# A mixture-of-experts kernel on Trainium2: the first expert weights laid out in the order in which they are fetched

## The chip, the cores and the metric

The kernel runs on one core of a Trainium2 chip. The metric is the device time of one execution in microseconds (us), as the median of several runs. The engines are PE (TensorE: matrix multiplies), DVE (VectorE), ACT (ScalarE), POOL (GpSimd) and SP (SyncE, which issues almost all transfers); 16 DMA engines move the data. All numbers are 32-bit floats unless said otherwise.

## What is computed

A batch of one, 256 tokens of width 1024, goes through two layers of a first model (three kinds of mixers and a dense feed-forward part) and then through one layer of a second model (attention and a recurrent mixer, then a mixture of 32 experts). The change touches the experts' weights alone. What they compute:

```python
def moe_ffn(h, ...):                     # h: 256 tokens x 1024
    logits = hf @ w_router + b_router    # 32 experts, the best 4 of each token
    ...
    def expert_block(args):
        xb, e = args
        gu = xb @ w_gu[e] + b_gu[e]      # w_gu[e]: 1024 x 2048, gate and up
        gate = jnp.minimum(gu[:, :D_EXPERT], SWIGLU_LIMIT)
        up = jnp.clip(gu[:, D_EXPERT:], -SWIGLU_LIMIT, SWIGLU_LIMIT)
        glu = gate * jax.nn.sigmoid(SWIGLU_ALPHA * gate)
        return ((up + 1.0) * glu) @ w_down[e] + b_down[e]   # w_down[e]: 1024 x 1024
    ...                                  # weighted by the gates and summed per token
```

"First weights" are `w_gu`, "second weights" `w_down`. The weights are inputs, and the program reads each expert's weights once: 32 x (8 + 4) MB.

## The kernel before

The first two layers and the second model's mixer come first, with their own weights. The last part, `moe`, goes over the 32 experts one after the other. Each expert has 24 units of weights, 512 KB each, a unit being one tile of 128 partitions x 1024 numbers: 8 units for each half `fh` of the first product (rows `kk` of 128, of the gate columns and of the up columns 512 each), then 8 units of second weights (rows of 128, all 1024 columns). `first` multiplies up to 64 gathered tokens with 8 units, `swiglu` applies the gate, `second` multiplies with the last 8, and the results of two experts are scattered back together. The experts at places 10, 16 and 22 in the order get 2, 1 and 1 extra blocks of 64 tokens (`HEAVY`, function `more`), which use the same units while they are held. Before the last expert stands a branch (`missing`, L2401) for tokens that found no place.

The units pass through a ring (`Ring`, from L1718). `ring_slots` lists the tiles of the earlier stages whose room is used again: 34 units in all (the tiles `rw2`, `rows`, `xh`, `xl`, `t`, `raw`, `hi`, `lo`, `mh`, `ml`, `cst1`; in the profile `rw`, `cst` and so on). `Ring.fill` is called after each group of matmuls and issues units up to 34 ahead. SP takes these issues in program order: each waits until PE has finished with the slot's former unit, and until the transfer eight before it has landed, since the transfers go over eight semaphores in turn. The experts' order is known only at run time; for every six experts `Ring.who` loads their numbers into registers of SP (L1754), and an issue adds the offset to the address. `Ring.fetch` issues one unit: for units 0 to 15 the source is 128 rows of `w_gu[e]`, of each row two pieces of 512 numbers (2 KB), 4 KB apart; for units 16 to 23 the source is 128 rows of `w_down[e]`, 1024 numbers (4 KB) each, one behind the other. `Ring.bias` issues an expert's 8 KB of biases.

The function `layout` prepares the inputs on the host, outside of the timed execution.

Of the kernel before, what the change touches and what calls it, by code (L numbers as in the profile page):

```python
# [20 lines left out]
P = 128  # L21
S = 256
D = 1024
KT = D // P
# [4 lines left out]
NE = 32  # L29
# [15 lines left out]
def _pair_rows(base):  # L45
    return np.concatenate([np.arange(base + h * 64, base + h * 64 + 64) for j in range(4) for h in PAIRS[j]])


def _in_columns():
    g, r, n = 0, 1040, 2096  # L50
    z = -1
    cols = []
    cols += list(range(r + 768, r + 896))
    cols += list(range(r + 896, r + 1024))
    cols += list(range(r + 1024, r + 1056))
    cols += list(range(g + 1024, g + 1040)) + [z] * 16
    cols += list(range(n + 1280, n + 1304)) + [z] * 8
    cols += list(range(3400, 3432))
    cols += list(range(r + 256, r + 512))
    cols += list(range(r, r + 256))  # L60
    cols += list(range(r + 512, r + 768))
    cols += list(range(g, g + 512))
    cols += list(range(g + 768, g + 1024))
    cols += list(_pair_rows(n))
    cols += list(range(n + 512, n + 768))
    cols += list(range(n + 768, n + 896))
    cols += list(range(n + 1024, n + 1152))
    cols += list(range(g + 512, g + 768))
    cols += list(range(n + 896, n + 1024))
    cols += list(range(n + 1152, n + 1280))  # L70
    return np.array(cols)
# [146 lines left out]
def _blocks(w):  # L218

    return np.ascontiguousarray(w.reshape(KT, P, -1, P).transpose(2, 1, 0, 3))  # L220


def layout(inp):
    inp = {k: np.asarray(v) for k, v in inp.items()}
    cols = _in_columns()
    o = {}
    o["xtm"] = inp["x"][0]
    o["xT"] = np.ascontiguousarray(inp["x"][0].T)
    for l in range(2):
        w = np.concatenate([inp["w_in"][l], inp["w_in_vres"][0] if l else np.zeros((D, 32), np.float32),  # L230
                            np.zeros((D, 1), np.float32)], 1)[:, cols]
        o[f"win{l}"] = _blocks(w[:, :NFM * P])

        wt = w[:, NFM * P:].reshape(2, 4, P, 2, 256)
        o[f"wtm{l}"] = np.ascontiguousarray(wt.transpose(3, 0, 2, 1, 4))
        gu = np.stack([inp["ffn_w_gate"][l].reshape(D, NFB, P), inp["ffn_w_up"][l].reshape(D, NFB, P)], 2)
        o[f"wgu{l}"] = _blocks(gu.reshape(D, 2 * FF))
        o[f"wdn{l}"] = np.ascontiguousarray(inp["ffn_w_down"][l])
        rows = np.concatenate([np.arange(512), _pair_rows(512)])
        o[f"wo{l}"] = np.ascontiguousarray(inp["w_out"][l][rows])  # L240
        o[f"wc{l}"] = np.ascontiguousarray(np.stack([inp["nsa_wk1"][l], inp["nsa_wv1"][l]]))
        o[f"pos{l}"] = np.concatenate([inp["nsa_pos_k"][l].reshape(16, P), inp["nsa_pos_v"][l].reshape(16, P)], 0)
        o[f"rows{l}"] = np.stack([inp["gla_ln_w"][l], inp["gla_ln_b"][l], inp["rwkv_ln_w"][l], inp["rwkv_ln_b"][l]])
        o[f"ln{l}"] = np.stack([inp["ln1_w"][l], inp["ln1_b"][l], inp["ln2_w"][l], inp["ln2_b"][l]])
    c2 = np.concatenate([_pair_rows(0), np.arange(512, 1792)])
    o["win2"] = _blocks(inp["w_in_2"][0][:, c2])
    rows = np.concatenate([_pair_rows(0), np.arange(512, 1024)])
    o["wo2"] = np.ascontiguousarray(inp["w_out_2"][0][rows])
    o["wada"] = inp["w_ada_2"][0]
    o["bada"] = inp["b_ada_2"]  # L250
    o["g3"] = np.stack([inp["g_mix_2"][0], inp["g_ffn_2"][0], inp["g_final_2"]])
    o["wgu"] = inp["w_gu_2"][0]
    o["wdn"] = inp["w_down_2"][0]

    o["bgu"] = np.ascontiguousarray(inp["b_gu_2"][0].reshape(NE, 2, KT, P).transpose(0, 3, 2, 1).reshape(NE, P, KT * 2))
    o["bdn"] = inp["b_down_2"][0]
    pr, _ = params(inp)
    o["pfm"] = np.ascontiguousarray(np.concatenate(pr.parts, 1))
    o["cst"] = np.ascontiguousarray(np.concatenate(CONST.parts, 1).astype(np.float32))
    return o, pr  # L260
# [1457 lines left out]
class Ring:  # L1718
# [37 lines left out]

    def fetch(self, w, u, es):
        k, d = self.k, self.k.d
        if u < 16:
            fh, kk = divmod(u, KT)  # L1760
            src = d["wgu"][es, kk * P:(kk + 1) * P, :].rearrange("o p (g f c) -> f (o p) g c", g=2, f=2)[fh]
            k.nc.sync.dma_start(w.rearrange("p (g c) -> p g c", g=2), src)
        else:
            k.nc.sync.dma_start(w, d["wdn"][es, (u - 16) * P:(u - 15) * P, :].rearrange("o p c -> (o p) c"))

    def bias(self, b, es):

# [804 lines left out]
```

## Time and profile before

| | |
|---|---|
| time, median of 3 runs | 2018.57 us (2015.73 to 2022.04) |
| the profiled execution | 2017.36 us, span 2015.6 us |
| PE / DVE / ACT / POOL busy in it | 1856.2 / 954.7 / 536.2 / 495.5 us |
| DMA | 571.82 MB in 234584 packets, 284 GB/s over the span |
| shares of the chain that ended last | PE 43%, DMA 21%, DVE 5%, ACT 3%, POOL 3% |
| mean granted TensorE clock | 0.968 of full speed |

The span runs from the first to the last instruction of the profiled execution; the execution's own time holds some 2 us more. Busy time is summed over stages that have different limits, so a share of the span says little about any one stage. The DMA share is the mean busy share of the 16 DMA engines; it passes 1 where the records of packets overlap. The chain is followed back from the last instruction: at each step to what released it.

### The profile page before, as it was taken

The numbers are of one execution on the slowest core, as the hardware profiler recorded it, in microseconds if no ns is written. First come the engines' busy times: TensorE is split into PE (matmuls) and PEld (weight loads), VectorE is DVE, ScalarE is ACT, GpSimd is POOL, SyncE is SP. The second block draws the span as 40 slices with busy tenths as digits, with TensorE's granted clock in tenths as the row PEclk, the third lists the DMA queues.
The fourth block names the chain that finished last, engine by engine and source line by source line (L and its number), as shares of the span: only waits on it lengthen the run. The fifth ranks groups of instructions, "written<-read, shape, count | busy, mean of one in ns | idle before, by whom it ended". The sixth has DMA issues, their size and how long they took to land.

```text
span 2015.6 us, 32453 instructions
## 1 busy us (share of the span) xinstructions
PE 1856.2 (92%) x12219; PEld 1137.0 (56%) x12219; DVE 954.7 (47%) x1705; ACT 536.2 (27%) x977; POOL 495.5 (25%) x425
## 2 busy tenths in 40 slices
PE   8989999999998999898799988999999999999886
PEld 7867899888867998697333322333333323332222
DVE  3656777667566776667433222233323322332222
ACT  4424444444343444364311100101111101110011
POOL 2434499234552995204200000000000000000000
PEclk9889999999898999998799999999999999999998
DMA  7420578754314778457899999969999999999997
GB/s 273 158 77 31 185 271 274 247 168 138 106 53 148 245 264 290 146 168 237 328 390 395 391 392 392 390 226 393 392 394 390 394 390 391 392 382 394 390 393 268
DMA packets 234584, 571.82 MB, mean 284 GB/s; under 512 B 22179, under 2 KB 31843, under 8 KB 234421
## 3 DMA queue, kind: packets, MB, share of 16 engines
q1 hardware_dynamic: 234420, 569.68, 78.0%
q8 instruction: 98, 1.61, 0.3%
q14 instruction: 66, 0.53, 0.1%
HBM read 568.54 MB, written 1.07 MB: 283 GB/s over the span
## 4 chain that ended last, share of the span: by engine, by line
PE 43%; DMA 21%; DVE 5%; ACT 3%; POOL 3%; issue 2%; SPq 0%; POOLq 0%; ACTq 0%; DVEq 0%
PE ps L385 41%; DMA raw<-wgu 4%; DMA t<-wgu 3%; DVE t L318 3%; DMA lo<-wgu 2%; PE ps L389 2%; ACT t L318 2%; DMA hi<-wgu 1%; POOL acc L318 1%; DMA cst<-wgu 1%; DMA mh<-wgu 1%; DVE lo L318 1%; DMA mh<-wdn 1%; DMA ml<-wgu 1%; POOL ada L318 1%
## 5 line engine op out<-in xcount | busy, mean ns | idle before, releaser
L385 PE MATMUL ps<-t,t 128*128 128x128 bf16 (+13 forms) x3912 | 452.0, 324 | 34.4 <-DVE t L318 12.2
L318 DVE TENSOR_TENSOR lo<-raw,hi 128x1024 fp32r<-128x1024 f32 x187 | 296.3, 1607 | 152.8 <-ACT hi L318 152.6
L318 ACT COPY t<-ps 128x512 f32<-128x512 f32 (+4 forms) x196 | 101.3, 525 | 861.6 <-PE ps L385 791.7
L385 PE MATMUL ps<-xh,hi 128*128 128x256 f32 x1184 | 310.5, 297 | 10.7 <-ACT hi L318 10.7
L385 PE MATMUL ps<-xh,lo 128*128 128x256 f32 x1184 | 305.5, 293 | 13.0 <-DVE lo L318 13.0
L385 PEld LDWEIGHTS ps<-t,t 32*32 32x32 f32 (+4 forms) x3000 | 176.1, 141 | 212.7 <-issue 119.4
L318 POOL TENSOR_SCALAR t<-t 128x1 f32<-128x1 f32 (+2 forms) x24 | 9.9, 411 | 1162.8 <-DVE t L318 1162.6
L318 DVE TENSOR_TENSOR t<-ps,pfm 128x512 f32<-128x512 f32 (+1 forms) x108 | 74.4, 688 | 414.0 <-PE ps L389 228.5
L318 ACT CAST hi<-raw 128x1024 fp32r<-128x1024 f32 x224 | 229.3, 1048 | 101.4 <-PE ps L385 50.8
L385 PEld LDWEIGHTS ps<-xh,lo 128*128 128x128 f32 x1184 | 238.2, 201 | 17.5 <-DVE lo L318 15.9
L385 PEld LDWEIGHTS ps<-xh,hi 128*128 128x128 f32 x1184 | 238.1, 201 | 15.5 <-ACT hi L318 10.9
L385 PE MATMUL ps<-xl,hi 128*128 128x256 f32 x1184 | 167.9, 285 | 0.0
L318 DVE TENSOR_TENSOR x<-x,ps 128x512 f32<-128x512 f32 x80 | 54.3, 686 | 212.9 <-PE ps L385 212.8
L385 PEld LDWEIGHTS ps<-xl,hi 128*128 128x128 f32 x1184 | 155.0, 195 | 0.0
L318 POOL TENSOR_TENSOR acc<-acc,ada 128x1024 f32<-128x1024 f32 x48 | 127.1, 2647 | 5.6 <-DMA acc<-bada 1.8
L318 POOL TENSOR_TENSOR lo<-raw,hi 128x1024 fp32r<-128x1024 f32 x37 | 93.3, 2522 | 125.6 <-ACT hi L318 102.8
L318 POOL TENSOR_SCALAR ada<-ada,cpar 128x1024 f32<-128x1024 f32 x48 | 114.6, 2387 | 36.7 <-DMA ada<-wada 36.6
L385 PE MATMUL ps<-hi,t 128*64 128x512 f32 x424 | 100.1, 599 | 3.7 <-DMA hi<-wgu 3.7
L385 PE MATMUL ps<-raw,t 128*64 128x512 f32 x416 | 97.9, 598 | 4.5 <-DMA raw<-wgu 4.1
L385 PE MATMUL ps<-lo,t 128*64 128x512 f32 x416 | 97.1, 597 | 3.2 <-DMA lo<-wgu 3.2
L389 PE MATMUL ps<-cst,t 128*128 128x128 f32 x524 | 85.1, 281 | 11.9 <-ACT t L318 9.5
L389 PEld LDWEIGHTS ps<-cst,t 128*128 128x128 f32 x524 | 58.4, 142 | 63.4 <-issue 34.2
(190 smaller groups left out, 2202.7 us busy)
## 6 DMA issues: line engine op xcount, KB each, us to landing
raw<-wgu SPq DMA_DIRECT2D x148, 512.0 KB, 5.6
t<-wgu SPq DMA_DIRECT2D x122, 512.0 KB, 10.5
raw<-wdn SPq DMA_DIRECT2D x76, 512.0 KB, 10.1
raw<-win SPq DMA_DIRECT2D x60, 512.0 KB, 4.3
hi<-wgu SPq DMA_DIRECT2D x60, 512.0 KB, 9.4
t<-wdn SPq DMA_DIRECT2D x58, 512.0 KB, 10.0
lo<-wgu SPq DMA_DIRECT2D x56, 512.0 KB, 10.6
ada<-wada SPq DMA_DIRECT2D x48, 512.0 KB, 4.3
```

Of the source, the lines that this page charges most:

```text
L318: r = f(*args, **kw)
L385: self.clk.note("PE", "mm", [out, lhsT, rhs], cost, self.nc.tensor.matmul(out, lhsT, rhs, start=start, stop=stop, skip_group_check=True))
L389: self.clk.note("PE", "tr", [out, in_], 110.0, self.nc.tensor.transpose(out, in_, ident))
```

## The change

The host lays out the first weights so that each unit is one run of 512 KB, in which each partition's 1024 numbers (512 of the gate, 512 of the up columns) lie one behind the other. The dimensions become expert, unit (`fh` outside, `kk` inside), partition, number. `w_down` is only given the same four dimensions; its bytes stay where they are. `Ring.fetch` then takes a unit by its number, with one form for both kinds. A transfer of first weights now reads 128 pieces of 4 KB where it read 256 pieces of 2 KB. The order of instructions on every engine, the slots, the waits and the registers are the same as before; lines behind the edit have other numbers.

```diff
-    o["wgu"] = inp["w_gu_2"][0]
-    o["wdn"] = inp["w_down_2"][0]
+
+    o["wgu"] = np.ascontiguousarray(inp["w_gu_2"][0].reshape(NE, KT, P, 2, 2, 512).transpose(0, 4, 1, 2, 3, 5)).reshape(NE, 16, P, 1024)
+    o["wdn"] = inp["w_down_2"][0].reshape(NE, KT, P, D)
...
     def fetch(self, w, u, es):
         k, d = self.k, self.k.d
-        if u < 16:
-            fh, kk = divmod(u, KT)
-            src = d["wgu"][es, kk * P:(kk + 1) * P, :].rearrange("o p (g f c) -> f (o p) g c", g=2, f=2)[fh]
-            k.nc.sync.dma_start(w.rearrange("p (g c) -> p g c", g=2), src)
-        else:
-            k.nc.sync.dma_start(w, d["wdn"][es, (u - 16) * P:(u - 15) * P, :].rearrange("o p c -> (o p) c"))
+        src = d["wgu"][es, u] if u < 16 else d["wdn"][es, u - 16]
+        k.nc.sync.dma_start(w, src.rearrange("o p c -> (o p) c"))
```

## Rows read from the trace of the kernel before

**Rows 1.** The page's 40 slices: busy tenths of the DMA engines, and GB/s.

```profile
DMA  7420578754314778457899999969999999999997
GB/s 273 158 77 31 185 271 274 247 168 138 106 53 148 245 264 290 146 168 237 328 390 395 391 392 392 390 226 393 392 394 390 394 390 391 392 382 394 390 393 268
```

**Rows 2.** The chain of waits, 900 to 2016 us: start, duration, what.

```profile
1021.05 9.80 PE ps L385 x80
...
1123.31 9.80 PE ps L385 x80
...
1138.88 11.37 DMA raw<-wgu
...
1258.47 3.87 PE ps L385 x52
...
1466.17 9.80 PE ps L385 x80
...
1548.38 9.80 PE ps L385 x80
...
1579.98 11.41 DMA lo<-wgu
...
1687.36 1.10 PE ps L385 x4
...
1799.35 7.96 DMA raw<-wgu
...
1969.92 6.25 DMA xh<-wgu
1976.29 9.19 PE ps L385 x32
```

**Rows 3.** Stretches of the expert stage: busy times; last, PEclk, DMA share, GB/s.

```profile
1008.00:1258.00 250.00, 234.33 (x1154) 80.29 (x1150) 71.68 (x148) 24.33 (x47) 4.96 (x4) 1.00 1.04 392
1258.00:1332.00 74.00, 68.94 (x386) 27.13 (x386) 20.63 (x44) 9.35 (x18) 0.00 (x0) 1.00 1.03 388
1332.00:1351.00 19.00, 17.96 (x74) 5.94 (x72) 7.04 (x12) 0.74 (x2) 0.00 (x0) 1.00 0.02 9
1351.00:1969.00 618.00, 586.76 (x3026) 210.52 (x3022) 174.58 (x366) 63.30 (x124) 0.00 (x0) 1.00 1.04 390
```

**Rows 4.** DMA queues over 1612–1620, 1629–1637, 870–875, 500–505, 630–635 us.

```profile
DMA packets 1634, 3.08 MB, mean 385 GB/s; under 512 B 138, under 2 KB 138, under 8 KB 1633
q1 hardware_dynamic: 1633, 3.06, 104.2%
...
DMA packets 979, 3.28 MB, mean 410 GB/s; under 512 B 101, under 2 KB 101, under 8 KB 979
q1 hardware_dynamic: 979, 3.28, 103.5%
...
DMA packets 702, 2.01 MB, mean 401 GB/s; under 512 B 62, under 2 KB 62, under 8 KB 702
...
DMA packets 1552, 1.86 MB, mean 371 GB/s; under 512 B 68, under 2 KB 1437, under 8 KB 1552
...
DMA packets 568, 1.71 MB, mean 342 GB/s; under 512 B 61, under 2 KB 189, under 8 KB 568
q1 hardware_dynamic: 568, 1.71, 99.0%
```

**Rows 5.** SP's issues in order of time: start, duration, engine, transfer, count.

```profile
988.37 0.54 SPq L318 DMA_DIRECT2D rows<-wgu  x1
...
1032.06 0.33 SPq L318 DMA_DIRECT2D rows<-wdn  x1
...
1324.80 26.38 SPq L318 DMA_DIRECT2D hi<-wgu  x4
```

**Rows 6.** Waits of SP's queue: us in total, times, longest.

```profile
SPq L318 <- DMA t<-wgu: 73.7, 113, 1.5
```

**Rows 7.** PE's loads of weights behind the branch, in order of time, with the idle time.

```profile
1976.26 0.32 PEld L385 LDWEIGHTS ps<-t,t 128*64 128x64 f32 x4 [7.57 <-PEq L2401]
```

## The prediction

> **What bounds the kernel now.** I read the 40 slices first, to find where the transfers are at their limit. From slice 21 on (about 1008 us) the 16 DMA engines are busy nine tenths or more in all slices but two, the one at the seventh place of that stretch and the last, and move about 390 GB/s [rows 1]. That is the expert stage; before it the rate never stays there. Next the chain of waits, to see whether the end hangs on those transfers. In the expert stage it changes hands six times [rows 2]: PE until 1138.9, transfers until 1258.5, PE until 1580.0, transfers until 1687.4, PE until 1799.4, transfers until 1976.2, then PE to the end. The reader should see two paces in it. Where PE leads, the same piece (9.80 us, x80) comes back every 51.13 us (1021.05, 1123.31 with one between): two experts, 25.57 us each. Where an expert has an extra block of tokens it takes longer: 82.21 us from 1466.17 to 1548.38, so 31.1 us for one extra block. The transfers' pace follows from the view by stages [rows 3]: at 392 GB/s an expert's 24 units of 524,288 bytes take 32.1 us. PE is thus faster by 6.5 us per expert. It lives off the ring of 34 units, runs it empty, and waits; each expert with extra blocks (10, 16, 22) lets the ring fill again. Once it fills to the brim: the queue stands still from 1332 to 1351 [rows 3], in one issue of four units that takes 26.38 us [rows 5].
>
> Last I looked at what the queue moves at which rate, in stretches in which nearly all pieces have one size [rows 4]. Over 1612 to 1620 it is the first weights: 1633 pieces for 3.06 MB (138 of them tiny), about 2 KB each, 385 GB/s. Over 1629 to 1637 it is mostly second weights, 4 KB pieces: 979 pieces, 410 GB/s. Both at a DMA share above 1, so in neither did the engines lack work.
>
> **The change, part by part.** No instruction is added, removed or moved on any engine: the same 768 units go to the same slots in the same order, PE reads the same bytes. What changes is the source of 512 of them (16 per expert): 256 pieces of 2 KB become 128 of 4 KB, as the 256 units of second weights have now.
>
> *A unit of first weights.* Now 524,288 B / 385 GB/s = 1.362 us. For the new form I take the rate of the units that already have it, 410 GB/s: 1.279 us. The difference is 0.083 us. Bounds: the other stretch with almost only 4 KB pieces lies in the first layer's stage, 401 GB/s [rows 4], which gives 1.307 us and a difference of 0.055; below that, nothing, if piece size is not the cause (a rival). I take 410 because it is the same stage, the same queue depth and the same kind of source; 0.055 goes to the range.
>
> *How many of them lie on the path.* Two stretches.
> - From 1008 to 1258 the queue never stops: 250 us x 392 GB/s = 98.0 MB, 187 units, two thirds of them first weights: 125. 125 x 0.083 = 10.3 us. They make expert 10 begin earlier. PE could go along: it needs 51.1 us for two experts, and the new transfers would take 48 x 1.279 = 61.4, so transfers stay the later ones.
> - From 1258 to 1351 PE leads while the ring fills and then stands. Nothing is gained here: the 74 us of transfers are covered by PE's extra blocks. The queue restarts when PE frees a slot, so its restart moves with PE, by 10.3 us. If that cover were gone, these units would be worth 74 x 388 / 524 = 55 units, 37 x 0.083 = 3 us.
> - From 1351 to 1969 it never stops again: 618 us x 390 GB/s = 241 MB, 460 units, 306 first weights, 306 x 0.083 = 25.4 us.
> - The units fetched before 1008 lie behind PE's own chain up to 1138.9: nothing (at most some 36 units, 3 us, if it were otherwise).
> - SP's issue of a unit: 0.54 us now, 0.33 for the 4 KB form [rows 5]. Nothing: SP waits for landings of earlier units before it issues (113 times for one tile alone, 0.65 us each [rows 6]), so a shorter issue only lengthens that wait. These waits also show what is late next if a unit came slower: the issue behind it.
>
> *What may eat some of it: the ring.* Gain that PE can't use at once, as in the PE stretches 1351 to 1580 and 1687 to 1799, stays as units ahead, unless the ring is full. At 1351 it holds 34. To 1540 the queue brings 189 us x 390 / 524 = 140 units; PE eats (189 - 31.1) / 25.57 = 6.2 experts, 148 units: 26 are left. The change adds 140 x 2/3 x 0.083 / 1.279 = 6, so 32 of 34. At the end of expert 22 the like could be a few more if PE took nothing of the gain between; four units over would cost 4 x 1.279 = 5 us. I count nothing for it and give 5 us to the range.
>
> *The end.* After the last transfer wait PE loses 7.57 us at the branch ahead of the last expert [rows 7] and then runs alone for 27 us; neither changes.
>
> **Sum.** 10.3 + 25.4 = 35.7 us off the profiled execution: span 2015.6 to 1979.9, its own time 2017.4 to 1981.7. The median of the runs, 2018.57, lies 1.2 above that execution, so for a median: **1983 us**.
>
> **The rivals.**
>
> *Only part of the difference is piece size.* The stretch 500 to 505 moved 1.86 MB in 1552 - 68 pieces, 1253 bytes each, at 371 GB/s [rows 4]. Each engine moves a sixteenth, so such a piece takes 54.0 ns and one of 2 KB (at 385) 85.1 ns; the line through these two has 5.0 ns per piece, and puts 4 KB at 165.2 ns, 397 GB/s. A unit would save 0.040 us, 431 units 17 us: 2001. Against it: 410 is measured on 4 KB pieces themselves, and that short stretch is a mix. Chance 0.06. The Trainium skill, DMA: Bandwidth & Descriptors, "Why small descriptors are slow (HBM only)", gives a fixed cost of about 3 cycles per packet beside one cycle per 32 B; by it two pieces of 2 KB take 134 cycles where one of 4 KB takes 131, an estimate of 2.2%, 13 us in all and 2006. The step from 385 to 410 is 6%, so the trace shows more than that rule.
>
> *No change.* Either the pieces stay 2 KB, or the 385 belongs to the first weights for another reason than their piece size (where they lie in memory, say), and goes with them: then 2018.6. For it: nothing but that the two rates come from different tensors. Against it: the three sizes, 1.2, 2 and 4 KB, stand in the order 371, 385, 410, and the second weights show that such a source is moved in 4 KB pieces. Chance 0.04. The Trainium skill, DMA: Bandwidth & Descriptors, "Specifications", has 512 B as the size from which transfers reach line rate, by which 2 KB pieces lose nothing and this rival would hold; the rows of three sizes speak against it.
>
> *Slower.* 4 KB pieces are not fast everywhere: over 630 to 635, with most of the bytes in pieces of 4 KB, the queue was at a share of 0.99 and moved 342 GB/s [rows 4]. If the first weights, packed without gaps, were read at that pace, a unit would take 1.533 us, 0.171 more than now, 431 x 0.171 = 74 us: 2092. It decides from the point where their rate falls under 385. Against it: the second weights are packed in the same way and show 410; that slow stretch is one in which the queue has just restarted with small parameter loads among the units. Chance 0.03.
>
> **How the numbers follow.** The forecast gets 0.87. Its own range goes from 0.055 per unit (23.7 us saved: 1995) with up to 5 us lost to a full ring, 2000, to 0.083 with the 3 us of the early units and the spread of the runs (2015.7 to 2022.0, some 3 us either way) on top: 1976. The range, 1975 to 2000, leaves out the rivals, 0.13, and little else. About 0.3% (6 us) is what a measurement of this kernel can tell from no change. Faster: 0.87 + 0.06 = 0.93; same: 0.04; slower: 0.03.
>
> **What would show it.** In the changed profile: 512 x 128 = 65,536 fewer DMA packets (234,584 to 169,048) at the same bytes; issues of first weights on SP at 0.33 us; a mean of about 407 GB/s in the saturated stretches; expert 10 reached some 10 us earlier; the standstill after it a little longer than 19 us, since the ring fills sooner; PE's 51.1 us per pair unchanged; the last transfer wait near 1940 instead of 1976. I am wrong if saturated stretches of first weights stay at 385, if a second standstill appears after expert 16 or 22, or if PE's pace changes.

## The result, and the profile after

The changed kernel takes 1983.70 us in the median of 4 runs (1982.29 to 1987.74), beside 2018.17 for the kernel before in its 4 runs. The ratio is 0.9843, with a 95% interval from 0.9822 to 0.9866. Forecast was 1983, within 1975 to 2000. Timed once more beside some of the experiments, the changed kernel took 1984.99 us in the median of 5, a ratio of 0.9828 (0.9810 to 0.9846).

| | before | after |
|---|---|---|
| span of the profiled execution | 2015.6 us | 1981.7 us |
| DMA packets | 234,584 | 169,047 |
| bytes moved | 571.82 MB | 571.82 MB |
| DVE / ACT / POOL busy | 954.7 / 536.2 / 495.5 us | 953.5 / 536.6 / 495.1 us |

The 40 slices of the page after (DMA busy tenths, GB/s):

```profile
DMA  7420578744322787736799999969999999999996
GB/s 270 158 87 21 172 259 277 265 150 149 130 76 99 237 271 252 253 139 208 267 405 407 408 408 407 409 250 379 408 407 408 408 407 406 404 401 408 402 408 261
```

Against [rows 1], the saturated slices stand at 401 to 409 GB/s where they stood at 382 to 395, all but the slice behind the standstill, which has 379. The slice with the standstill (the seventh of the stage) is still there. The stages after, cut as those of [rows 3] (busy times, then PEclk, DMA share, GB/s):

```profile
1008.00:1258.00 250.00, 242.30 (x1246) 87.79 (x1242) 73.97 (x153) 26.52 (x51) 4.97 (x4) 1.00 1.03 408
1258.00:1320.00 62.00, 57.21 (x298) 21.64 (x298) 18.38 (x39) 7.19 (x14) 0.00 (x0) 1.00 1.01 397
1320.00:1339.00 19.00, 17.96 (x74) 5.94 (x72) 7.04 (x12) 0.74 (x2) 0.00 (x0) 1.00 0.01 4
1339.00:1940.00 601.00, 578.59 (x3028) 214.76 (x3024) 176.09 (x368) 63.35 (x124) 0.00 (x0) 1.00 1.02 405
```

408 for 392 in the first, 405 for 390 in the last. SP's issues after, in order of time (start, duration):

```profile
989.16 0.33 SPq L319 DMA_DIRECT2D rows<-wgu  x1
...
1312.12 27.53 SPq L319 DMA_DIRECT2D hi<-wgu  x4
```

A unit of first weights is issued in 0.33 us, as units of second weights were [rows 5]. The issue that spans the standstill ends at 1339.65, where it ended at 1351.18: the first part of the gain, 11.5 us. The first row shows that the changed kernel comes to this stage 0.8 us later (989.16, where it was 988.37), so within the stage the gain is 12.3 us. The queue over the same 1612 to 1620 us as in [rows 4], now in pieces of 4 KB:

```profile
DMA packets 901, 3.28 MB, mean 410 GB/s; under 512 B 100, under 2 KB 100, under 8 KB 901
```

PE in order of time, two equal places of the scattering of two experts' sums, and the first weight load behind the branch (at the end, the idle time ahead of it):

```profile
1376.37 1.98 PE L386 MATMUL ps<-t,t 128*128 128x512 f32 x4
...
1427.50 1.98 PE L386 MATMUL ps<-t,t 128*128 128x512 f32 x4
...
1942.00 0.33 PEld L386 LDWEIGHTS ps<-t,t 128*64 128x64 f32 x4 [7.60 <-PEq L2398]
```

PE's pace is what it was: 51.13 us for two experts. It comes out of the branch at 1942.00 where it came out at 1976.26 [rows 7], 34.3 us earlier, and loses 7.60 us there as before. From there to the end of the span it takes 39.7 us, where it took 39.3.

Last, what PE still waits for transfers, by the page's groups (busy, mean ns, then idle time ahead and its main releaser). The first row is the page before, the second the page after:

```profile
L385 PE MATMUL ps<-hi,t 128*64 128x512 f32 x424 | 100.1, 599 | 3.7 <-DMA hi<-wgu 3.7
```

```profile
L386 PE MATMUL ps<-hi,t 128*64 128x512 f32 x424 | 99.0, 597 | 1.7 <-DMA hi<-wgu 1.5
```

The wait for this tile fell to less than half. Over the whole last stretch of the stage, PE is idle for 22.4 of 601 us where it was for 31.2 of 618.

### The profile page after: what moved, and what is told of

It reads as the page before. It is cut to its first block, busy times and chain, and to the rows that moved or that the text cites. A ratio compares the mean times of both kernels' runs of the same rounds, so it can differ in the third digit from the quotient of the medians.

```text
span 1981.7 us, 32453 instructions
## 1 busy us (share of the span) xinstructions
PE 1845.2 (93%) x12219; PEld 1143.0 (58%) x12219; DVE 953.5 (48%) x1705; ACT 536.6 (27%) x977; POOL 495.1 (25%) x425
## 2 busy tenths in 40 slices
DMA packets 169047, 571.82 MB, mean 289 GB/s; under 512 B 22178, under 2 KB 31842, under 8 KB 168884
## 5 line engine op out<-in xcount | busy, mean ns | idle before, releaser
L386 PE MATMUL ps<-xh,lo 128*128 128x256 f32 x1184 | 301.6, 291 | 12.4 <-DVE lo L319 12.3
L386 PEld LDWEIGHTS ps<-t,t 32*32 32x32 f32 (+4 forms) x3000 | 180.8, 144 | 202.0 <-issue 126.2
```

Of the source, the lines that this page charges most:

```text
L386: self.clk.note("PE", "mm", [out, lhsT, rhs], cost, self.nc.tensor.matmul(out, lhsT, rhs, start=start, stop=stop, skip_group_check=True))
```

## The experiments

Theory: the engines that move the data spend a fixed time per piece, so the size of the pieces sets the rate in the stretches in which PE waits for it. Rivals: it is the run without gaps in memory that helps; the slow rate belongs to the tensor; SP's shorter issue gains the time.

**One run of 512 KB, but pieces of 2 KB.** Host layout and fetch:

```diff
-    o["wgu"] = np.ascontiguousarray(inp["w_gu_2"][0].reshape(NE, KT, P, 2, 2, 512).transpose(0, 4, 1, 2, 3, 5)).reshape(NE, 16, P, 1024)
+    o["wgu"] = np.ascontiguousarray(inp["w_gu_2"][0].reshape(NE, KT, P, 2, 2, 512).transpose(0, 4, 1, 3, 2, 5)).reshape(NE, 16, 2, P, 512)
...
+            k.nc.sync.dma_start(w.rearrange("p (g c) -> p g c", g=2), d["wgu"][es, u].rearrange("o g p c -> (o p) g c"))
...
```

> The changed kernel, but each unit of first weights, still one run of 512 KB in memory, is stored with the gate half of all partitions ahead of the up half, so it is read in 256 pieces of 2 KB again. Theory (the pace of the engines is set by the size of the pieces): back to the kernel before, 2018 us (2012 to 2024), 234,584 packets, 385 GB/s where first weights flow. Rival (the run without gaps is what helped, not the size of a piece): as the changed kernel, 1984 us, some 408 GB/s.

Measured: 2014.99 us, ratio 0.9986 (0.9969 to 1.0002): the kernel before. Its queue over 1612 to 1620 (first weights) and 1598 to 1602 (second weights), and one issue of each kind:

```profile
DMA packets 1674, 3.05 MB, mean 381 GB/s; under 512 B 199, under 2 KB 199, under 8 KB 1672
...
DMA packets 448, 1.64 MB, mean 410 GB/s; under 512 B 48, under 2 KB 48, under 8 KB 448
```

```profile
988.25 0.37 SPq L319 DMA_DIRECT2D rows<-wgu  x1
...
1030.61 0.33 SPq L319 DMA_DIRECT2D rows<-wdn  x1
```

The gain is gone although each unit lies without gaps. And the issue of a unit fell to 0.37 us, nearly as short as after the change, without any gain: this one run rejects the run without gaps and SP's issue at once.

**Second weights in pieces of 2 KB**, first weights as changed:

```diff
-    o["wdn"] = inp["w_down_2"][0].reshape(NE, KT, P, D)
+    o["wdn"] = np.ascontiguousarray(inp["w_down_2"][0].reshape(NE, KT, P, 2, 512).transpose(0, 1, 3, 2, 4))
...
+            k.nc.sync.dma_start(w.rearrange("p (g c) -> p g c", g=2), d["wdn"][es, u - 16].rearrange("o g p c -> (o p) g c"))
```

> The changed kernel, with the second weights stored in the same way, so that they, 256 units, are read in pieces of 2 KB while the first weights keep 4 KB. Theory: a third of some 646 units in saturated stretches, 215, lose 0.075 to 0.083 us each, 16 to 18 us: 2000 to 2002 us; the rate of second weights falls to 385 GB/s while first weights stay near 410. Rival (the slower rate belonged to the first weights' tensor and went with their new layout): second weights stay at 410, 1984 us.

Measured: 1998.06 us, ratio 0.9899 (0.9874 to 0.9925), 13 to 14 us over the changed kernel, where 16 to 18 were expected, and 2 us under the expected 2000 to 2002. The queue over 1608 to 1616 (first weights, 4 KB) and 1627 to 1631 (second weights, 2 KB):

```profile
DMA packets 974, 3.24 MB, mean 405 GB/s; under 512 B 188, under 2 KB 188, under 8 KB 973
...
DMA packets 801, 1.54 MB, mean 386 GB/s; under 512 B 47, under 2 KB 47, under 8 KB 801
```

The two rates have changed places with the piece sizes. The tensor is not what made the rate.

**First weights in pieces of 1 KB** (four quarters, each of all partitions):

```diff
-    o["wgu"] = np.ascontiguousarray(inp["w_gu_2"][0].reshape(NE, KT, P, 2, 2, 512).transpose(0, 4, 1, 2, 3, 5)).reshape(NE, 16, P, 1024)
+    o["wgu"] = np.ascontiguousarray(inp["w_gu_2"][0].reshape(NE, KT, P, 2, 2, 2, 256).transpose(0, 4, 1, 3, 5, 2, 6)).reshape(NE, 16, 4, P, 256)
...
+            k.nc.sync.dma_start(w.rearrange("p (g c) -> p g c", g=4), d["wgu"][es, u].rearrange("o g p c -> (o p) g c"))
...
```

> The changed kernel, with the first weights stored so that they are read in pieces of 1 KB. Theory with a fixed cost per piece from the 2 KB and 4 KB rates (85.1 and 159.8 ns per engine: 10.4 ns a piece): a piece of 1 KB takes 47.7 ns, 343 GB/s, a unit 1.53 us, 0.165 more than at 2 KB; 27 experts of saturated time at 16 units: 2018 + 71 = 2089 us (2075 to 2105). Rival (5.0 ns a piece, the line through the pieces of 1.2 and 2 KB): 45.1 ns, 364 GB/s, 2018 + 34 = 2052 us.

Measured: 2080.63 us, ratio 1.0307 (1.0279 to 1.0335), within the theory's range and 28 us over the rival with 5.0 ns a piece. Over 1612 to 1620:

```profile
DMA packets 2799, 2.79 MB, mean 349 GB/s; under 512 B 81, under 2 KB 2798, under 8 KB 2798
```

349 GB/s, where 343 were expected. A sixteenth of the rate is one engine's: 46.9 ns for 1 KB, 85.1 for 2 KB (at 385), 159.8 for 4 KB (at 410). The steps are 38.2 ns for one KB more and 74.7 for two more, so about 37 to 38 ns for each KB, and 9 to 10 ns that every piece costs whatever its size. The traces' own records of packets, which overlap by 3 to 10 per cent, agree: over 1612 to 1620 a piece of 1 KB takes 51 ns in this run, one of 2 KB 88 ns in the kernel before, one of 4 KB 163 ns in the changed kernel, and the tiny pieces of 4 bytes among them 9 to 10 ns each.

**Two transfers of 64 partitions for each unit**, pieces of 4 KB as in the changed kernel:

```diff
...
+        for h in (slice(0, 64), slice(64, P)):
+            k.nc.sync.dma_start(w[h, :], src[h, :])
```

> The changed kernel, but each unit is fetched by two transfers of 64 partitions, in pieces of 4 KB as before: SP issues twice as many transfers, and the eight semaphores hold half as many bytes in flight. Theory (the engines' pace bounds, SP and the depth of the queue have slack): 1984 to 1995 us, DMA share 1.0 and near 400 GB/s in the saturated stretches. Rival (SP's shorter issue, 0.33 us instead of 0.54, was what gained): two issues cost at least 0.12 us per unit more than one of 0.54, so slower than the kernel before, over 2030 us.

Measured: 2665.77 us, ratio 1.3226 (1.3197 to 1.3255). Far off the theory, and the time lies on the rival's side; but not for its reason. The queue over 1500 to 1520, the stretch 1400 to 1800, and a row of SP's waits (total, times, longest):

```profile
DMA packets 1414, 4.65 MB, mean 232 GB/s; under 512 B 284, under 2 KB 284, under 8 KB 1412
q1 hardware_dynamic: 1412, 4.62, 103.7%
```

```profile
1400.00:1800.00 400.00, 299.69 (x1328) 93.82 (x1330) 71.31 (x149) 28.21 (x55) 0.00 (x0) 0.89 1.03 232
```

```profile
SPq L319 <- DMA t<-wgu: 108.1, 226, 1.3
```

SP waits for landings here too, and the engines' share stands at 1.03: they are never short of work, but move 232 GB/s. By the records of packets a piece of 4 KB takes 290 ns over 1500 to 1520. What differs from the changed kernel is the partitions of a transfer, the number of issues, and the bytes in flight. The next run keeps the last two.

**Two transfers of all 128 partitions**, half of the numbers each:

```diff
...
+        for h in (slice(0, 512), slice(512, 1024)):
+            k.nc.sync.dma_start(w[:, h], src[:, h])
```

> The changed kernel, but each unit of either kind is fetched by two transfers of all 128 partitions, 512 numbers (2 KB) of each: as many issues and as few bytes in flight as with two transfers of 64 partitions, which took 2666 us. Theory (it is the 64 partitions that slowed the engines there; SP's issues and the depth have slack): pieces of 2 KB throughout, 385 GB/s, so the kernel before and its second weights at 2 KB: 2018 + 18 = 2036 us (2025 to 2060). Rival (twice the issues, or half the bytes in flight, slowed it): about 2600 us again.

Measured: 2059.50 us, ratio 1.0211 (1.0191 to 1.0230), at the upper end of what was expected. Its stretch 1400 to 1800:

```profile
1400.00:1800.00 400.00, 390.53 (x1946) 145.97 (x1946) 113.58 (x237) 40.66 (x81) 0.00 (x0) 1.00 1.03 370
```

Twice the issues and half of the bytes in flight cost some of the rate (370, where 385 were expected), nothing like the fall to 232. So that fall came with the 64 partitions. Why the engines move such a transfer slower wasn't tried.

**Pieces of 8 KB where the ring has double tiles.** The host stores units in pairs, and a double tile is filled by one transfer:

```diff
...
+        n = w.shape[1] // 1024
+        src = d["wgu"][es, u // 2] if u < 16 else d["wdn"][es, u // 2 - 8]
+        c = u % 2 * 1024
+        k.nc.sync.dma_start(w, src.rearrange("o p c -> (o p) c")[:, c:c + n * 1024])
```

> The changed kernel, with the weights stored in pairs of units; the five ring tiles that hold two units (10 of 34 units) are filled by one transfer of 1 MB in pieces of 8 KB, the other tiles in pieces of 4 KB that stand 8 KB apart. Theory with 10.4 ns a piece (fitted to 2 and 4 KB; 1 KB came out as it says): 8 KB take 309 ns, 424 GB/s, a unit 1.236 us, 0.043 less; 646 units of saturated time x 10/34 x 0.043 = 8 us: 1976 us. Rival (a piece over 4 KB is moved as two of 4 KB): as the changed kernel, 1984 us, with as many packets as it.

Measured: 1981.33 us, ratio 0.9811 (0.9792 to 0.9830), beside 0.9828 (0.9810 to 0.9846) for the changed kernel timed beside it on the same chip. From the page, and two stretches:

```profile
DMA packets 152917, 571.79 MB, mean 289 GB/s; under 512 B 20387, under 2 KB 30051, under 8 KB 138421
```

```profile
1008.00:1240.00 232.00, 224.24 (x1140) 82.31 (x1136) 69.53 (x143) 24.79 (x49) 4.96 (x4) 1.00 1.03 411
...
1345.00:1930.00 585.00, 569.43 (x3004) 214.93 (x3000) 174.70 (x366) 63.36 (x124) 0.00 (x0) 1.00 1.02 408
```

Some 14,500 packets now have 8 KB or more, so the pieces did grow, and the saturated rates are 411 and 408 for 408 and 405. In time it is 3.7 us by the medians, where 8 were expected, and the intervals overlap: a gain isn't settled.

**Half of the first weights.** Only the first 512 numbers of each unit are fetched, and the up half's matmuls read the gate half's weights, so this kernel leaves out half of the first weights:

```diff
...
+            k.nc.sync.dma_start(w[:, 0:512], d["wgu"][es, u].rearrange("o p c -> (o p) c")[:, 0:512])
...
-                k.mm(o[u * 64:u * 64 + 64, :], x(kk), w[:, u, :], start=kk == 0, stop=kk == KT - 1)
+                k.mm(o[u * 64:u * 64 + 64, :], x(kk), w[:, 0, :], start=kk == 0, stop=kk == KT - 1)
```

> The changed kernel, but of each unit of first weights only the first 512 numbers of each partition are fetched, and the matmuls of the up half read the gate half's weights (this leaves out half of the first weights; the instructions on PE are as many). Theory (between its waits for transfers PE keeps 25.55 us per expert, and the waits that are left are 14.6 us ahead of expert 10 and 18 us at experts 26 to 30): 1984 - 33 = 1951 us (1946 to 1956). Rival (PE is itself slowed by the transfers beside it, or the ring's releases become a wait): PE's pace differs from 51.1 us per pair, and the time lies outside of that.

Measured: 1941.61 us (1940.61 to 1944.23), ratio 0.9624 (0.9609 to 0.9640): 42 to 43 us under the changed kernel, 4 below the range. A stretch in which PE had waited for transfers, two around the branch, and PE's restart behind it:

```profile
1040.00:1240.00 200.00, 199.38 (x1054) 77.28 (x1052) 62.61 (x131) 22.82 (x44) 0.00 (x0) 1.00 0.95 331
...
1900.00:1904.00 4.00, 4.00 (x22) 1.20 (x18) 0.02 (x1) 0.00 (x0) 0.00 (x0) 1.00 0.04 10
1904.00:1907.00 3.00, 2.07 (x10) 0.74 (x10) 1.38 (x2) 0.00 (x0) 0.00 (x0) 1.00 0.33 90
```

```profile
1905.27 0.23 PEld L386 LDWEIGHTS ps<-t,t 128*64 128x64 f32 x4 [1.78 <-PEq L2400]
1905.30 1.94 PE L386 MATMUL ps<-t,t 128*64 128x512 f32 x8 [0.93 <-PEq L2400]
```

PE no longer waits (199.38 of 200 us busy), and the transfer waits were worth about what was expected: the restart comes 1942.00 - 1905.27 = 36.7 us earlier, of which 5.8 are at the branch (1.78 us idle for 7.60), so 30.9 of waits for 32.6. What was not expected is the branch's part, and no low clock stands behind it (1.00 over 1904 to 1907). In the changed kernel the same place reads:

```profile
1943.00:1946.00 3.00, 3.00 (x10) 0.99 (x8) 0.00 (x0) 0.00 (x0) 0.00 (x0) 0.50 0.95 359
```

From the restart to the end of the span it is 37.1 us there (1905.27 to 1942.4) and 39.7 in the changed kernel (1942.00 to 1981.7).

**The branch behind the last expert**, where no weights are in flight:

```diff
-        if e == NE - 1:
-            missing()
...
+    missing()
     norms = []
...
```

> The changed kernel, with the branch for tokens without a place moved from ahead of the last expert to behind it, where no weights are in flight. Theory (ahead of the last expert PE loses 7.6 us at the branch, whose new code arrives among the weights, and then runs some 5 us at half the clock; behind it the branch costs about the 3.5 us that it took in the run with half of the first weights, beside the last sums): 5 to 8 us less than the changed kernel, 1977 to 1980 us. Rival (the branch costs as much wherever it stands): 1984 us.

Measured: 1983.65 us, ratio 0.9844 (0.9819 to 0.9868), five runs from 1979.2 to 1992.4: no gain that can be told, where 5 to 8 us were expected. The profiled execution is the fastest of the five and takes 4.3 us less than the changed kernel's. PE's last matmuls of the last expert and its restart behind the branch:

```profile
1955.08 2.13 PE L386 MATMUL ps<-hi,t 128*64 128x512 f32 x8 [1.08 <-DMA hi<-wdn]
1957.40 1.08 PE L386 MATMUL ps<-hi,t 128*64 128x512 f32 x4 [0.19 <-DMA hi<-wdn]
1958.65 1.08 PE L386 MATMUL ps<-hi,t 128*64 128x512 f32 x4 [0.17 <-DMA hi<-wdn]
...
1963.48 5.37 PE L386 MATMUL ps<-t,t 128*128 128x512 f32 x8 [3.75 <-PEq L2398]
```

The restart behind the branch ahead of the last expert, in the changed kernel:

```profile
1942.03 3.68 PE L386 MATMUL ps<-t,t 128*64 128x512 f32 x8 [6.75 <-PEq L2398]
```

Three things ate into the gain. Without the pause PE catches up with the transfers of the last units and waits for them. The branch still costs 3.75 us; by the same measure, the idle time of PE's matmuls, it costs 6.75 us in the changed kernel and 0.93 us in the run with half of the first weights, where the expectation took 3.5 us from that run. And the eight matmuls behind it take 5.37 us at a mean clock of 0.72 (1963 to 1969), where the changed kernel's last eight took 3.71.

**Both at once** (double tiles and the branch behind):

> Both at once: the branch behind the last expert, and the five double tiles of the ring filled by one transfer in pieces of 8 KB. Theory (the two are independent; pieces of 8 KB gave 3.7 us by the medians of their run, though within its interval): 3 to 5 us less than with the branch alone, 1973 to 1976 us. Rival (pieces of 8 KB bring nothing): as with the branch alone.

Measured: 1981.84 us, ratio 0.9831 (0.9812 to 0.9851), 1.8 us under the branch alone by medians, within the interval; 1973 to 1976 were expected. Apart from the run that leaves out half of the first weights, no version beats the changed kernel by more than the runs scatter.

## Why the prediction was right

- **The bound.** Right: the saturated stretches rose from 392 and 390 to 408 and 405 GB/s, PE's pace stayed at 51.13 us per pair, and the time followed the transfers. Halving the first weights' bytes took away the waits that were left.
- **A unit of first weights.** The price of 0.083 us holds where the queue is undisturbed (410 GB/s over 1612 to 1620). Over the long stretches it was less. From 1339 to 1940, 601 us x 405 GB/s are 464 units at 1.295 us; before it was 618 us for 460 units, 1.344. The difference, 0.049 per unit of either kind, is 0.073 per unit of first weights. No run shows why the mean lies under the best stretch.
- **The bounds.** The lower one, 0.055 us, was read from a row that does not show it. In the row of 870 to 875 us [rows 4] the 640 pieces that are not tiny hold 2.01 MB, 3.1 KB each, so they are not almost only pieces of 4 KB. SP had just issued four units of the experts' first weights, in pieces of 2 KB, ahead of units of the second model's mixer (not the first layer's):

```profile
861.95 1.99 SPq L318 DMA_DIRECT2D rw<-wgu  x3
863.99 1.15 SPq L318 DMA_DIRECT2D rows<-wgu  x1
865.46 11.95 SPq L318 DMA_DIRECT2D raw<-win  x5
```

That 401 GB/s is the rate of a mix, and that the 0.073 measured lies above 0.055 is luck. The 410 had better ground: over 1629 to 1637 some 3.7 KB come on each piece that is not tiny, and the changed kernel shows 410 with pieces of 4 KB alone.

- **The two terms.** The first, forecast at 10.3 us, measured 11.5 at the end of the standstill, 12.3 within the stage. The second, forecast at 25.4, measured 34.3 - 11.5 = 22.8. The first came out 2 us too small, the second 2.6 too large, and that the sum came so close is in part luck. In the second the 306 units were right, and 306 x 0.073 = 22.3 is what came: using the best stretch's rate for the whole of it was the flaw. The sum was 35.7. Measured are 12.3 + 22.8 = 35.1 us within the stage; less 0.8 at its start and 0.4 at the end that is 33.9 for the span, and the median fell by 34.5.
- **Costed at nothing.** SP's issue: shown, since pieces of 2 KB with an issue of 0.37 us run like the kernel before. The units fetched before 1008: not nothing, it seems. The stretch 1008 to 1258 alone gives 9.8 us by its rates (its 98.0 MB at 408 GB/s instead of 392), so some 2 of the 12.3 us came from outside of it; how many of them from those units the runs don't part. A full ring: no second standstill, the last stretch stays at 405 GB/s.
- **The standstill** takes 27.53 us in one issue of four units for 26.38, a little longer, as forecast.
- **The rivals.** "Only part of the difference is piece size" (397 GB/s for 4 KB) is refuted by 410 and by the run with 1 KB. "No change" fell with the result, and its reason with the swap of rates between the two tensors. "Slower" had its row in an earlier stage; nothing of it appeared in this one. By the 3 cycles per packet of the Trainium skill, DMA: Bandwidth & Descriptors, "Why small descriptors are slow (HBM only)", the change would have been worth 13 us, an estimate that leaves out the 32 bytes of descriptor data per operation which the section names beside them; the runs show a cost per piece of 9 to 10 ns and 34 us.

## What to carry to other kernels

Where transfers are what the work waits for, compare the rate of neighbouring transfers that differ in piece size: the better rate, which the kernel already reaches, tells what a new layout gives, and the units that move in saturated stretches tell how often. Take the mean over a long stretch for that rate, not its best eight microseconds. Then ask how much waiting is left: by the run with half of the first weights it is some 40 us here with the branch, so the next few per cent of transfer rate bring less than they did now.

## What the runs showed that was not expected

- Transfers of 64 partitions, in the same pieces of 4 KB, kept the DMA engines at a share of 1.03 and moved 232 GB/s, while 128 partitions moved 370 with as many issues and pieces of half the size. The cause is open.
- The branch ahead of the last expert costs PE 7.60 us while weights fill the queues, and 1.78 us where they are idle (a share of 0.04 over 1900 to 1904); after the long pause PE runs at 0.50 of its clock (1943 to 1946), that is its lower level of 1.2 GHz. That the weights in flight delay the branch fits both runs, but moving the branch to an idle queue left 3.75 us of idle matmuls (6.75 ahead of the last expert, 0.93 in the run with half of the first weights), so it is not shown to be the whole of it.
